# The gate products of the RG-LRU branch in the four quarters of TensorE's array

## The chip, the cores and the metric

The kernel runs on one core of a Trainium2 chip. The metric is the device time of one execution in microseconds (us). An execution is one launch of the whole network; the host only lays the data out.

## The reference

The network has two layers over 512 tokens (256 of context, 256 latent), 1024 features wide, in float32. A layer is a feed-forward half step, a mixer of three branches that run beside each other (SSD, RG-LRU and GLA), and a second feed-forward half step. The change touches the RG-LRU branch alone. Its input x, after a convolution over four tokens, is cut into 16 blocks of 64 channels. In each of two directions every block has two gates:

```
xb = x.reshape(x.shape[:-1] + (16, 64))
r = sigmoid(einsum('btnk,nkj->btnj', xb, w_a[d]).reshape(x.shape) + b_a[d])
i = sigmoid(einsum('btnk,nkj->btnj', xb, w_x[d]).reshape(x.shape) + b_x[d])
log_a = -8 * r * softplus(-lam[d])
a, b = exp(log_a), sqrt(-expm1(2 * log_a)) * (i * x)      # h[t] = a[t] * h[t-1] + b[t]
```

So there are 64x64 weight matrices, 16 of them for each gate and each direction, d = 0 forward in time and d = 1 backward. The sum of both scans times the gelu of a second input is the branch's output.

## The kernel before

Features lie on the 128 partitions and tokens along a page of 512 columns, so a tile is 128 channels, that is two blocks of the RG-LRU; there are eight tiles in a layer. The big products (`proj`, `mm3`, L360 to L365) are three matmuls each: weights and inputs are split into a rounded part and the exact rest. The weights stream in through SyncE's DMA queue; ScalarE rounds a tile of them (L333), VectorE takes the rest (L334), and TensorE reads both. A projection is 24 such matmuls into one of eight PSUM banks.

Everything smaller is background work: Python generators in a list (`start`, L755). After each projection `pump` (L774) advances them, in the list's order, until the pieces' stated costs use up a budget: 5.0 for projections of all 512 columns, 2.5 for those of the latent half alone (L799). A `yield c` ends a piece of cost c, and a `yield None` ends that generator's turn. `need` (L784) runs what is left at once. Three of the eight banks belong to background work (`B`, L208): a bank is taken from the front of the list of free ones and put back at its end. The instructions that come out so are then ordered for each engine by a planner, on its own estimates of when operands and banks are ready; so background matmuls can stand between two matmuls of a projection. On the chip each engine works through its list in order and waits where something isn't ready.

`lru_batch` (L861) is the generator changed here; one runs for two tiles. For each tile it loads the weights (L867), ends its turn, and takes four pages. Then for each direction d and each gate k it takes a bank, makes one product (L874) and one sigmoid with bias out of that bank into a page (L875), and puts the bank back; a piece ends after each direction. The 64x64 blocks of the tile's two blocks stand on the diagonal of a 128x128 matrix whose other half is zeros (`host_arrays`, L1650 to L1655). After both tiles come a tanh (L885), a product on GpSimd (L886), a square root (L890), an exponential (L894), the scans on VectorE (L909 to L914), the sum of directions (L916), the gelu's factor (L918) and the split into two parts (`hilo`, L853) that the branch's output product reads (`merge`, L1329, from the string ORDER's entry M0 on).

In layer 0 the mixer works on all columns; in layer 1 the outputs are wanted for the latent half alone, but the gates and scans of this branch still run over all 512 columns.

Of the kernel before, what the change touches and what calls it, by code (L numbers as in the profile page):

```python
# [15 lines left out]
P = 128  # L16
# [68 lines left out]
class Half:  # L85
    """Half of a page that stands for the latent columns of a whole one."""
# [10 lines left out]
class Prog:  # L97
# [9 lines left out]
    # ---------------------------------------------------------------- memory  # L107
# [42 lines left out]
    def press(self, pages, n):  # L150
        """Background work is brought forward until n pages are free."""
        while len(pages) < n and self.bg:
            t = next((t for t in self.bg if not t[2]), None)
            if t is None:
                break
            self._advance(t)
# [44 lines left out]
    def Fc(self, c0):  # L201
        """A page for the columns from c0."""
        return self.half(self.F) if c0 else self.F()
# [16 lines left out]
    def behind(self, x, first):  # L220
        """x is queued behind first, whose start flag clears all of the bank's accumulation bits."""
        if not self.dry:
            self.tc.add_manual_dep(x.ins, first.ins.name, NOSYNC, reason="same bank")
# [6 lines left out]
    # ---------------------------------------------------------------- streams  # L230
# [7 lines left out]
    def raw_issue(self, n=10 ** 6):  # L238
        """Transfers up to number n into free slots."""
        while not self.dry and self.raw_free and self.issued < min(n, len(self.plan)):  # L240
            j = self.issued
            t = self.raw_free[0]
            if j >= self.first_of.get(self.until, 10 ** 6):
                t = next((x for x in self.raw_free if all(x is not y for y in self.extra[0])), None)
                if t is None:
                    break
            self.raw_free = [x for x in self.raw_free if x is not t]
            self.raw_of[j] = t
            self.nc.sync.dma_start(self.raw_of[j], self.a["ws"][j].rearrange("p (b c) -> p b c", b=8))
            self.issued += 1  # L250

    def raw_next(self, what):
        """The next transfer's slot; raw_done follows once its reads are queued."""
        i = len(self.seq)
        self.seq.append(what)
        if self.dry:
            return Any()
        assert self.plan[i] == what, (i, self.plan[i], what)
        self.raw_issue()
        return self.raw_of[i]  # L260
# [22 lines left out]
    def more_slots(self, raw, spl):  # L283
        """Further slots, for the rest of the phase."""
# [10 lines left out]
    def retire(self):  # L295
        """The extra slots are not used again."""
# [7 lines left out]
    def pair(self, ps):  # L304
        """A weight slot from a pair of double pages."""
        return tuple(x if self.dry else x.rearrange("p a (b c) -> p (a b) c", c=P) for x in ps)

    def split_ahead(self, n):
        """Parts of the next weight tiles, tiles before number n being done: hi rounded to float32r, lo the exact rest."""
# [32 lines left out]
    def W(self, *specs, hold=0):  # L342
        """The next blocks of the weight stream, side by side: hi and lo, [128, 128 * n] each.
        hold: how many weight tiles before this one are still to be read."""
# [22 lines left out]
    # ---------------------------------------------------------------- ada  # L367
# [7 lines left out]
    def ada_first(self, q):  # L375
        """Products for shift and scale of the first layer's input, two tiles of each."""
# [12 lines left out]
    def first_u(self, q, t):  # L389
        """The modulations from those products, and the first layer's input with them, in parts."""  # L390
# [21 lines left out]
    def ffn_start(self):  # L412
        """The first six products of the first phase, contraction outermost, as the modulations come in."""
# [13 lines left out]
    def ada_begin(self, pool):  # L427
        """silu of the conditioning vectors, on every partition."""
# [8 lines left out]
    def ada_part(self, n=1):  # L437
        """n tiles of 128 modulation features each, from the rows of the transposed weights."""
# [16 lines left out]
    # ---------------------------------------------------------------- prologue  # L455
# [39 lines left out]
    # ---------------------------------------------------------------- residual and LayerNorm  # L495
    def res_begin(self, l, j, w, c0):
        """gate columns w * mods[3j + 2] for the sub-layer's output."""
# [9 lines left out]
    def res_tile(self, m, ps, halves):  # L507
        """z of tile m, from the sub-layer's output in PSUM."""
# [10 lines left out]
    def res_mean(self, halves):  # L519
        """From every z the mean over the features of its first tile is taken off; LayerNorm is blind to it."""  # L520
# [33 lines left out]
    def ln_prep(self):  # L554
        """Next modulation folded with the LayerNorm's scale and shift."""
# [16 lines left out]
    def ln_sums(self, i):  # L572
        """Sums over the tiles before the last, of half i's columns."""
# [7 lines left out]
    def ln_stats(self, i):  # L581
        """Mean and 1 / sqrt(var + eps) of half i's columns, in acc and sq[0]."""
# [22 lines left out]
    def ln_apply(self, i, q):  # L605
        """The LayerNorm over z tiles 2q and 2q + 1 of half i; then u with the next modulation, if any."""
# [34 lines left out]
    def set_cuts(self, c0):  # L641
        """The halves in use of the columns, each with its own conditioning."""
        self.halves = (1,) if c0 else (0, 1)

    def tail(self, spec, src, n):
        """The last n output tiles of a sub-layer, of the one half of the columns and then of the other."""
# [32 lines left out]
    # ---------------------------------------------------------------- first products of a phase  # L679
    def k_outer(self, spec, starts, pre):  # L680
        """Four output tiles, contraction outermost; the latent columns lag by two weight tiles."""
# [19 lines left out]
    # ---------------------------------------------------------------- feed-forward  # L701
# [4 lines left out]
    def ffn(self, l, j, c0, jm, ps=None):  # L706
        """Sub-layer jm (0 or 2) of layer l with feed-forward weights j; columns from c0 on."""
# [46 lines left out]
    # ---------------------------------------------------------------- background work  # L754
# [5 lines left out]
    def _advance(self, t):  # L760
        """One piece; its cost in microseconds of the busier vector engine, or None at a break."""
# [27 lines left out]
    # ---------------------------------------------------------------- projections  # L789
    def proj(self, specs, src, c0, ps=None, mid=None):  # L790
        """One output tile, [128 features, tokens from c0]: specs run over the contraction tiles src."""
# [17 lines left out]
    # ---------------------------------------------------------------- pieces  # L809
    def conv(self, y, ps, w, b, line, lo):  # L810
        """y = b + the four taps of ps along each line; w(k) and b are per-partition columns."""
# [13 lines left out]
    def silu2(self, out, ps, c0):  # L825
        """out = 2 silu(ps) = (tanh(ps / 2) + 1) ps"""
# [4 lines left out]
    def softplus(self, x, e, r, q, p):  # L831
        """x <- softplus(x), accurate for results near 0 too; e, r, q, p: scratch of x's shape."""
# [14 lines left out]
    def rms_scale(self, ps, n, out, c0, eps):  # L847
        """out = 1 / sqrt(ps / n + eps)"""
# [11 lines left out]
    # ---------------------------------------------------------------- RG-LRU  # L860
    def lru_batch(self, l, tiles, c0, out):  # L861
        """tiles: (number, convolved x, gelu of the gate)."""
        nc = self.nc
        st = []
        for t, xc, gl in tiles:
            w = self.F()
            nc.sync.dma_start(w, self.a["lw"][l][:, t])  # L867
            yield None
            rs = [self.F() for _ in range(4)]
            for d in range(2):  # L870
                for k, n in ((0, "lba"), (1, "lbx")):
                    ps = self.B()
                    c = (2 * d + k) * P
                    nc.tensor.matmul(ps, w[:, c:c + P], xc, start=True, stop=True)  # L874
                    nc.scalar.activation(rs[2 * d + k], ps, AF.Sigmoid,  # L875
                                         bias=self.par[l][:, PR[n] + d * 8 + t:PR[n] + d * 8 + t + 1])
                    self.fB(ps)
                yield 1.2
# [44 lines left out]
    # ---------------------------------------------------------------- SSD  # L923
    def ssd_dt(self, l, x):
        """From the biased dt rows [64 = 2 x 32, tokens]: softplus, decay sums, their columns, the sums in DRAM."""
# [189 lines left out]
    # ---------------------------------------------------------------- GLA  # L1115
    def gla_head(self, l, h, q, k, v, gs, alr, c0, out):
        """q, k: [dk, tokens]; v: per 128 tokens [tokens, 2 heads * dv]; gs: silu of the gate, 2 tiles."""
# [149 lines left out]
    # ---------------------------------------------------------------- the mixer  # L1267
# [10 lines left out]
    def mixer(self, l):  # L1278
# [18 lines left out]
        # RG-LRU  # L1297
# [28 lines left out]
        # merge  # L1326
# [60 lines left out]
        # RG-LRU and SSD, with the products of the RG-LRU branch between  # L1387
# [20 lines left out]
        # GLA, with the products of the SSD branch between  # L1408
# [92 lines left out]
    # ---------------------------------------------------------------- whole program  # L1501
    def consts2(self):
        """Per layer: 4 and -8 times softplus(-lam); the two directions' skips summed."""
# [73 lines left out]
def host_blocks(inp, specs):  # L1577
    """[128, 8, 128] of one stream tile."""
# [34 lines left out]
def feat(v):  # L1613
    """[..., n * 128] -> [128, ... * n]"""
# [4 lines left out]
def host_arrays(inp, seq):  # L1619
# [9 lines left out]
    for l in range(DEPTH):  # L1629
# [14 lines left out]
        put("lba", feat(inp["lru_b_a"][l]))  # L1644
        put("lbx", feat(inp["lru_b_x"][l]))
# [4 lines left out]
    lw = np.zeros((DEPTH, 2, 64, 8, 2, 2, 2, 64), np.float32)  # L1650
    for k, n in enumerate(("lru_w_a", "lru_w_x")):
        w = inp[n].reshape(DEPTH, 2, 8, 2, 64, 64)
        for b in range(2):
            lw[:, b, :, :, :, k, b] = w[:, :, :, b].transpose(0, 3, 2, 1, 4)
    lw = lw.reshape(DEPTH, P, 8, 4 * P)  # L1655
# [36 lines left out]
```

## Time and profile before

| | |
|---|---|
| median of 3 runs | 2749.73 us |
| lowest and highest | 2748.28 and 2752.57 us |
| profiled execution, first to last instruction (span) | 2746.5 us |
| TensorE matmuls busy | 2679.0 us, 98% |
| VectorE busy | 1935.4 us, 70% |
| ScalarE busy | 1221.4 us, 44% |
| GpSimd busy | 343.7 us, 13% |

The page gives the profiled execution's own time as its span only; the median of the runs, which were timed without a profile, is 3.2 us above that. In the rows below PE is TensorE, PEld its weight loads, DVE VectorE, ACT ScalarE, POOL GpSimd and SP SyncE; L874 is line 874 of the kernel. A float32 matmul shows as two records, a matmul on rounded parts as one. Matmuls are pipelined: the next one starts before the one before it ends, so the distance between starts tells more than a duration.

### The profile page before, as it was taken

What the parts mean: (1) busy time and instruction counts of PE and PEld (TensorE: products, weight loads), DVE (VectorE), ACT (ScalarE), POOL (GpSimd) and SP (SyncE); (2) the same over time, 40 slices, a digit from 0 to 9 for tenths busy, and PEclk for the clock granted to TensorE, in tenths of its full rate; (3) what the DMA queues carried; (4) which work ended last, traced back from release to release, by engine and by line L of the source; (5) the groups of instructions that cost most, each with busy time, mean ns of one, the idle gap of its engine ahead of it and who ended that gap; (6) DMA issues with size and microseconds to landing.
All of it is one profiled execution on the core that took longest, in us unless ns stands there. A gap on an engine that the chain in (4) does not pass through costs nothing.

```text
span 2746.5 us, 38825 instructions
## 1 busy us (share of the span) xinstructions
PE 2679.0 (98%) x14981; PEld 2280.9 (83%) x14981; DVE 1935.4 (70%) x3465; ACT 1221.4 (44%) x1745; POOL 343.7 (13%) x295
## 2 busy tenths in 40 slices
PE   7999999999999999999999999999999999999997
PEld 5888897677887888888888898888977798899997
DVE  4788769599985545458888587733598998676654
ACT  2332326863435434333323242232388655574553
POOL 0000132212210000022000230001311112002002
PEclk9999999999999999999999999999999999999999
DMA  6566534234342222234566436533333454344563
GB/s 258 184 191 195 182 122 128 71 104 138 123 135 85 74 85 77 85 103 150 185 198 199 154 108 196 180 108 107 97 117 113 135 171 132 107 139 130 169 192 116
DMA packets 117832, 380.49 MB, mean 139 GB/s; under 512 B 13888, under 2 KB 22352, under 8 KB 117648
## 3 DMA queue, kind: packets, MB, share of 16 engines
q1 hardware_dynamic: 115744, 373.00, 42.4%
q0 software_dynamic: 1472, 4.33, 0.5%
q8 instruction: 117, 1.92, 0.3%
q10 hardware_dynamic: 432, 0.69, 0.1%
q14 instruction: 67, 0.55, 0.1%
HBM read 373.63 MB, written 4.33 MB: 138 GB/s over the span
## 4 chain that ended last, share of the span: by engine, by line
PE 82%; DVE 8%; ACT 5%; issue 3%; DMA 1%; POOL 1%; SPq 0%; DVEq 0%; POOLq 0%; ACTq 0%
PE bank L362 25%; PE bank L363 25%; PE bank L364 25%; DVE wl L334 1%; DVE x L822 1%; PE bank L1233 1%; PE bank L1213 1%; PE bank L1052 1%; PE bank L874 1%; PE bank L1018 1%; PE bank L1170 1%; ACT wh L333 1%; ACT x L875 1%; PE bank L1073 0%; DVE x L908 0%
## 5 line engine op out<-in xcount | busy, mean ns | idle before, releaser
L333 ACT ACTIVATE wh<-wr 128x1024 fp32r<-128x1024 f32 x391 | 413.3, 1058 | 762.1 <-PE bank L363 519.5
L334 DVE TENSOR_TENSOR wl<-wr,wh 128x1024 fp32r<-128x1024 f32 x391 | 487.8, 1248 | 264.8 <-ACT wh L333 263.0
L444 DVE SCALAR_TENSOR_TENSOR ada_scr<-wr,sb 128x1024 f32<-128x1024 f32 x256 | 315.6, 1233 | 138.5 <-DMA wr<-in_ws_dram 135.2
L362 PE MATMUL bank<-u0h,wh 128*128 128x512 f32 (+1 forms) x660 | 246.7, 376 | 7.2 <-ACT u0h L628 3.8
L362 PE MATMUL bank<-r,wh 128*128 128x512 f32 (+1 forms) x736 | 251.6, 342 | 0.0
L364 PE MATMUL bank<-r,wl 128*128 128x512 f32 (+1 forms) x736 | 249.7, 340 | 0.0
L363 PE MATMUL bank<-r,wh 128*128 128x512 f32 (+1 forms) x736 | 249.6, 339 | 0.0
L363 PE MATMUL bank<-u0l,wh 128*128 128x512 f32 (+1 forms) x660 | 236.8, 359 | 2.1 <-DVE u0l L630 2.0
L364 PE MATMUL bank<-u0h,wl 128*128 128x512 f32 (+1 forms) x660 | 237.9, 361 | 1.0 <-DVE wl L334 0.9
L362 PE MATMUL bank<-u1h,wh 128*128 128x512 f32 (+1 forms) x660 | 234.7, 358 | 3.2 <-ACT u1h L408 2.7
L363 PE MATMUL bank<-u1l,wh 128*128 128x512 f32 (+1 forms) x660 | 233.9, 355 | 0.8 <-DVE u1l L630 0.8
L364 PE MATMUL bank<-u1h,wl 128*128 128x512 f32 (+1 forms) x660 | 234.2, 355 | 0.0
L362 PE MATMUL bank<-u2h,wh 128*128 128x512 f32 (+1 forms) x660 | 233.1, 354 | 0.0
L363 PE MATMUL bank<-u2l,wh 128*128 128x512 f32 (+1 forms) x660 | 233.0, 353 | 0.1
L364 PE MATMUL bank<-u2h,wl 128*128 128x512 f32 (+1 forms) x660 | 232.9, 353 | 0.0
L363 PE MATMUL bank<-u3l,wh 128*128 128x512 f32 (+1 forms) x644 | 228.6, 355 | 1.3 <-DVE u3l L630 1.3
L362 PE MATMUL bank<-u3h,wh 128*128 128x512 f32 (+1 forms) x644 | 228.3, 356 | 0.0
L364 PE MATMUL bank<-u3h,wl 128*128 128x512 f32 (+1 forms) x644 | 228.1, 355 | 0.0
L362 PEld LDWEIGHTS bank<-r,wh 128*128 128x128 f32 x736 | 139.4, 190 | 16.1 <-issue 1.0
L362 PEld LDWEIGHTS bank<-u0h,wh 128*128 128x128 f32 x660 | 125.8, 192 | 32.1 <-issue 6.5
L364 PEld LDWEIGHTS bank<-r,wl 128*128 128x128 f32 x736 | 139.5, 190 | 15.4 <-issue 0.3
L363 PEld LDWEIGHTS bank<-r,wh 128*128 128x128 f32 x736 | 139.5, 190 | 14.8
(502 smaller groups left out, 5911.2 us busy)
## 6 DMA issues: line engine op xcount, KB each, us to landing
wr<-in_ws_dram SPq DMA_DIRECT2D x605, 512.0 KB, 3.7
m1r<-in_ws_dram SPq DMA_DIRECT2D x29, 512.0 KB, 4.0
ada<-in_ws_dram SPq DMA_DIRECT2D x16, 512.0 KB, 9.0
x<-acs_d SPq DMA_DIRECT2D x26, 256.0 KB, 3.6
x<-acs_d SPq DMA_DIRECT2D x45, 128.0 KB, 3.5
x<-in_lw_dram SPq DMA_DIRECT2D x16, 256.0 KB, 3.6
sb<-s_d SPq DMA_DIRECT2D x6, 512.0 KB, 5.8
f<-acs_d SPq DMA_DIRECT2D x19, 128.0 KB, 3.2
```

Source lines behind the costliest of these rows:

```text
L333: nc.scalar.activation(hi, raw, AF.Copy)
L334: nc.vector.tensor_tensor(lo, raw, hi, op=ALU.subtract)
L362: x = nc.tensor.matmul(out, st[0], mv[0], start=start, stop=False, skip_group_check=True)
L363: nc.tensor.matmul(out, st[0], mv[1], start=False, stop=False, skip_group_check=True)
L364: self.last_mm = nc.tensor.matmul(out, st[1], mv[0], start=False, stop=stop, skip_group_check=True)
L444: nc.vector.scalar_tensor_tensor(self.ada_scr, raw.rearrange("p a b -> p (a b)"), 1.0, self.sb[b], op0=ALU.mult, op1=ALU.mult, accum_out=o ...
L822: nc.vector.scalar_tensor_tensor(ys[:, :, a:z], xs[:, :, a + o:z + o], w(k), ys[:, :, a:z], op0=ALU.mult, op1=ALU.add)
L874: nc.tensor.matmul(ps, w[:, c:c + P], xc, start=True, stop=True)
L875: nc.scalar.activation(rs[2 * d + k], ps, AF.Sigmoid, bias=self.par[l][:, PR[n] + d * 8 + t:PR[n] + d * 8 + t + 1])
L1018: nc.tensor.matmul(cc(ps, c), cc(Bt, c), cc(xw[d], c), start=True, stop=True, skip_group_check=True)
L1052: nc.tensor.matmul(cc(ps, c)[s], cc(Sd[d], c)[:, s], cc(Cp, c), start=True, stop=True, skip_group_check=True)
L1170: nc.tensor.matmul(cc(ps, c), cc(ki[d], c), cc(qi[d], c), start=True, stop=True, skip_group_check=True)
```

## The change

A gate k of a tile now makes four products of 64 rows by 64 columns: the forward blocks of the two 64-channel halves lie in the quarters on the array's diagonal (rows 0 to 63 to columns 0 to 63, and 64 to 127 to 64 to 127) and write bank pf; the backward blocks lie in the other two quarters and write bank pb, each half to the partitions of the other. The forward gate is one sigmoid over all partitions. The backward gate is two sigmoids of 64 partitions, which write each half to its own partitions again. The weights hold no zeros any more, a transfer is 128 KB instead of 256 KB, and the backward biases are rolled by 64 partitions on the host. Pieces end after each gate instead of each direction, at a stated cost of 1.8 instead of 1.2. The comments and docstrings of the file are blank lines now, so that the line numbers shift by at most three.

```
     def lru_batch(self, l, tiles, c0, out):
...
-            nc.sync.dma_start(w, self.a["lw"][l][:, t])
+            nc.sync.dma_start(w[:, 0:256], self.a["lw"][l][:, t])
             yield None
             rs = [self.F() for _ in range(4)]
-            for d in range(2):
-                for k, n in ((0, "lba"), (1, "lbx")):
-                    ps = self.B()
-                    c = (2 * d + k) * P
-                    nc.tensor.matmul(ps, w[:, c:c + P], xc, start=True, stop=True)
-                    nc.scalar.activation(rs[2 * d + k], ps, AF.Sigmoid,
-                                         bias=self.par[l][:, PR[n] + d * 8 + t:PR[n] + d * 8 + t + 1])
-                    self.fB(ps)
-                yield 1.2
+            lo, up = slice(0, 64), slice(64, P)
+            for k, n in ((0, "lba"), (1, "lbx")):
+                pf, pb = self.B(), self.B()
+                for ps, d, ii, oo in ((pf, 0, lo, lo), (pf, 0, up, up), (pb, 1, lo, up), (pb, 1, up, lo)):
+                    c = (2 * d + k) * 64
+                    nc.tensor.matmul(ps[oo], w[ii, c:c + 64], xc[ii], start=True, stop=True, skip_group_check=True)
+                bias = lambda d, s: self.par[l][s, PR[n] + d * 8 + t:PR[n] + d * 8 + t + 1]
+                nc.scalar.activation(rs[k], pf, AF.Sigmoid, bias=bias(0, slice(0, P)))
+                for ii, oo in ((up, lo), (lo, up)):
+                    nc.scalar.activation(rs[2 + k][oo], pb[ii], AF.Sigmoid, bias=bias(1, ii))
+                self.fB(pf, pb)
+                yield 1.8
             self.fF(w)
...
-        put("lba", feat(inp["lru_b_a"][l]))
-        put("lbx", feat(inp["lru_b_x"][l]))
+        for n, k in (("lba", "lru_b_a"), ("lbx", "lru_b_x")):
+            b = feat(inp[k][l]).copy()
+            b[:, 8:] = np.roll(b[:, 8:], 64, axis=0)
+            put(n, b)
...
-    lw = np.zeros((DEPTH, 2, 64, 8, 2, 2, 2, 64), np.float32)
-    for k, n in enumerate(("lru_w_a", "lru_w_x")):
-        w = inp[n].reshape(DEPTH, 2, 8, 2, 64, 64)
-        for b in range(2):
-            lw[:, b, :, :, :, k, b] = w[:, :, :, b].transpose(0, 3, 2, 1, 4)
-    lw = lw.reshape(DEPTH, P, 8, 4 * P)
+    lw = np.stack([inp[n].reshape(DEPTH, 2, 8, 2, 64, 64) for n in ("lru_w_a", "lru_w_x")], axis=3)
+    lw = lw.transpose(0, 4, 5, 2, 1, 3, 6).reshape(DEPTH, P, 8, 4 * 64)
```

## Rows read from the trace of the kernel before

**Rows 1.** The page: busy time by engine, and the chain that ended last, by engine.

```profile
PE 2679.0 (98%) x14981; PEld 2280.9 (83%) x14981; DVE 1935.4 (70%) x3465; ACT 1221.4 (44%) x1745; POOL 343.7 (13%) x295
...
PE 82%; DVE 8%; ACT 5%; issue 3%; DMA 1%; POOL 1%; SPq 0%; DVEq 0%; POOLq 0%; ACTq 0%
```

**Rows 2.** The chain of waits by line: 430 to 630 us, then 2005 to 2240 us.

```profile
by line: issue 12.3%; PE bank L362 7.6%; PE bank L364 7.4%; PE bank L363 7.4%; DVE x L822 5.7%; DVE wl L334 5.6%; ACT x L875 4.3%; PE bank L874 4.1%; DVE x L908 3.6%; ACT x L890 3.3%; DVE x L918 3.1%; DVE x L909 2.8%; DMA f<-acs_d 2.4%; ACT
...
by line: PE bank L362 11.2%; PE bank L363 10.7%; PE bank L364 10.6%; issue 7.1%; DVE x L822 6.4%; PE bank L874 4.7%; DVE wl L334 3.1%; DVE x L908 2.6%; DVE m1l L334 2.5%; DVE x L909 2.5%; ACT x L875 2.4%; PE bank L1018 2.4%; POOL x L916 2.2
```

**Rows 3.** Busy time of each engine in two slices of 30 us.

```profile
490.00:520.00 30.00, 28.80 (x113) 20.94 (x112) 12.20 (x18) 28.43 (x38) 5.16 (x5) 1.00 0.19 60
...
2050.00:2080.00 30.00, 28.65 (x149) 22.66 (x148) 21.87 (x41) 25.08 (x38) 6.97 (x5) 1.00 0.35 112
```

**Rows 4.** Groups by line: busy us, mean ns, idle us before and releasers.

```profile
L874 PE MATMUL bank<-x,x 128*128 128x512 f32 x128 | 64.0, 622 | 12.9 <-ACT x L953 4.9 <-ACT x L875 3.5 <-DVE x L990 3.2
...
L875 ACT ACTIVATE x<-bank,par 128x512 f32<-128x512 f32 x57 | 36.8, 686 | 6.2 <-PE bank L874 3.0 <-PE bank L364 2.2 <-POOL x L916 0.7
```

**Rows 5.** Timeline of TensorE: start us, us, line, shapes, count; gate products and projections.

```profile
436.84 2.73 PE L874 MATMUL bank<-x,x 128*128 128x512 f32 x6
...
440.73 1.12 PE L874 MATMUL bank<-x,x 128*128 128x512 f32 x2
...
446.04 3.59 PE L874 MATMUL bank<-x,x 128*128 128x512 f32 x8
...
449.70 0.40 PE L363 MATMUL bank<-u0l,wh 128*128 128x512 f32 x1
449.93 0.39 PE L364 MATMUL bank<-u0h,wl 128*128 128x512 f32 x1
...
2153.82 3.59 PE L874 MATMUL bank<-x,x 128*128 128x512 f32 x8
```

**Rows 6.** Timeline of TensorE around two groups of half-array products.

```profile
631.48 0.39 PE L364 MATMUL bank<-r,wl 128*128 128x512 f32 x1
631.80 1.09 PE L1073 MATMUL bank<-x,x 128*64 128x128 f32 x16
...
633.16 0.40 PE L362 MATMUL bank<-u0h,wh 128*128 128x512 f32 x1
...
639.07 0.39 PE L364 MATMUL bank<-u3h,wl 128*128 128x512 f32 x1
639.39 1.53 PE L1052 MATMUL bank<-x,x 128*64 128x128 f32 x24
...
641.19 0.40 PE L363 MATMUL bank<-r,wh 128*128 128x512 f32 x1
```

**Rows 7.** Single lines: count, duration ns min/median/max, first and last start.

```profile
L875 ACT ACTIVATE x<-bank,par x57: 671/687/699, 440.0 to 2149.4; 128x512 f32<-128x512 f32 x57
...
L1352 ACT ACTIVATE r<-bank x2: 590/590/591, 433.6 to 2009.2; 32x512 fp32r<-32x512 f32 x2
```

**Rows 8.** Waits of TensorE, 395 to 640 us: total us, times, longest.

```profile
PE bank L874 <- ACT x L875: 3.1, 2, 2.8
...
PE bank L362 <- ACT wh L333: 0.8, 1, 0.8
```

**Rows 9.** DMA issues: count, KB each, us to landing.

```profile
x<-in_lw_dram SPq DMA_DIRECT2D x16, 256.0 KB, 3.6
```

**Rows 10.** Timeline: last work of the branch, first product that reads it, per layer.

```profile
605.44 0.68 DVE L857 TENSOR_TENSOR r<-x,r 128x512 fp32r<-128x512 f32 x1
...
623.84 0.48 PE L362 MATMUL bank<-r,wh 128*128 128x512 f32 x1
...
2196.73 0.42 DVE L918 TENSOR_TENSOR f<-f,x 128x256 f32<-128x256 f32 x1
...
2221.05 0.28 PE L362 MATMUL bank<-r,wh 128*128 128x256 f32 x1
```

**Rows 11.** Timeline of TensorE: a gate product that waits for a bank.

```profile
479.95 2.07 PE L874 MATMUL bank<-x,x 128*128 128x512 f32 x2 [4.92 <-ACT x L953]
```

## The prediction

> **What bounds the kernel now.** I read the whole span first, then the stretches around the changed lines, then single instructions. TensorE is busy for 98% of the span, and 82% of the chain of waits is its own [rows 1], so time on TensorE is time of the kernel unless something else ends a stage. The changed code runs in two stretches, one per layer; its products (L874) start at 436.84 and end with a group at 2153.82 [rows 5]. There the picture differs. Of the chain from 430 to 630 us TensorE's projections (L362 to L364) hold only 22%, from 2005 to 2240 us 33%; the rest is split over VectorE, ScalarE and the gate products, with 4.3% (8.6 us) for the sigmoids' line L875 and 4.1% (8.2 us) for L874 [rows 2]. In the second stretch of 235 us it is 2.4% (5.6 us) and 4.7% (11.0 us) [rows 2]. TensorE is nearly full (28.80 and 28.65 us of 30 in the slices shown), and ScalarE not far from it (28.43 and 25.08) [rows 3]. So what the change takes from TensorE and what it gives to ScalarE weigh against each other in the same place.
>
> **TensorE, per product.** A product on L874 shows as two records (128 records, 64 products, four per tile of 128 channels, 16 tiles in both layers) [rows 4]. Eight records start at 446.04, and the second projection matmul behind them at 449.70; a projection matmul takes 0.23 us of the queue (449.70 to 449.93), so four products take 3.66 - 0.23 = 3.43 us, 0.86 us each [rows 5]. All 64 take 54.9 us; nothing is lost where they go in or out.
>
> A quarter product (64 rows, 64 columns) does not exist in this trace. The nearest rows are the half-array products of L1052 and L1073, 128 rows by 64 columns in alternate column halves. From the projection matmul before a group to the second one after it, less two times 0.23 us, the group of 16 records costs 633.16 - 631.48 - 0.45 = 1.23 us and the one of 24 records 641.19 - 639.07 - 0.45 = 1.67 us [rows 6]. Eight more records, which are two pairs of products, cost 0.44 us: 0.22 us a pair. A full-width product of these 128 columns would cost 0.86 / 4 = 0.21 us. So two column halves run at once, for the price of one. What is left, 1.23 - 4 x 0.22 = 0.35 us, is paid once per group for changing the shape of the array and back.
>
> Now the after side. A gate (forward and backward) becomes four quarter products of 512 columns. All at once they cost one step, 0.86 us, against 1.72 us now; as two pairs 1.72 us; one after the other 3.44 us. To this comes 0.35 us per group. I take all four at once: the quarters differ in rows or columns, the column half of this is shown above, and nothing in the trace shows the row half either way.
>
> **How the groups fall.** Background work has three PSUM banks. A product now fills one bank and the sigmoid frees it; a gate will fill two (pf, pb). A tile fills four banks before and after, and the fourth fill must wait for the first sigmoid. That is why many tiles show as six records, other work, then two (436.84 and 440.73, with ScalarE's L875 between) [rows 5]. In the timeline L874 comes in 30 groups: 5 of eight records, 7 of six, 5 of four, 13 of two. (The first and the last stand in [rows 5].) After the change such a split tile costs 0.86 + 0.86 + 0.35, later 0.86 + 0.35, together 3.28 us against 3.43 now: only 0.15 us less, because the last two quarters run without the other two. An unsplit tile costs 1.72 + 0.35 = 2.07 us: 1.36 less. A tile cut by gates costs 2.42: 1.01 less. One cut into four pairs costs 4.84: 1.41 more. Five unsplit tiles give -6.8, seven split -1.1; the other four (the groups of four and the loose twos) lie between -4.0 and +5.6, I take -1. Sum: **-9 us**, with bounds of -22 (all unsplit) and +23 (all in pairs).
>
> **ScalarE.** Per tile six sigmoids instead of four, since the backward halves go back across partitions in two instructions: 32 more. A sigmoid of 128 x 512 takes 0.687 us; a copy of 32 rows out of a bank to other partitions takes 0.590 [rows 7]. Fewer rows save little, so I take 0.64, the middle: 32 x 0.64 = +20.5 us of ScalarE. Below, it could cost nothing where ScalarE idles; above, all 20.5. Line L875 is busy for 36.8 us in its larger group, 57 of its 64 sigmoids [rows 4], so some 41 in all; 14.2 us of that stand on the chain [rows 2], a third. A third of 20.5 is **+7 us**. Queued behind the added sigmoids on ScalarE are the weight splits (L333) and behind these the projections; between 395 and 640 us TensorE already waits 0.8 us for L333 and 3.1 us for L875's release of a bank [rows 8].
>
> **The rest.** The weights' transfers shrink from 256 to 128 KB; they land in 3.6 us now [rows 9], and each is issued a pump ahead of its use: nothing. Each piece now counts 1.8 instead of 1.2 of the pump's budget, 9.6 more per layer: two pumps of 5.0 in layer 0, two to four in layer 1, where a pump has 2.5 or 5.0. A pump in layer 0 comes every 24 x 0.23 = 5.5 us, so the branch ends about 11 us later. What hides this is the gap between the last work of the branch and the first product that reads it: 606.1 to 623.8 us in layer 0, 2197.2 to 2221.1 us in layer 1 [rows 10]. Cover of 17 and 24 us; if it were gone, each microsecond over it would stand on the path. I cost it at nothing. Pages, banks and VectorE's work stay as they are. One accident near the change may go or come again: before 479.95 TensorE waits 4.92 us for a bank that L953 releases [rows 11]. In all TensorE idled 12.9 us before L874 [rows 4]; I expect as much again, give or take 8.
>
> **Sum.** -9 + 7 = -2 us. The profiled execution spans 2746.5 us, the median of the runs is 2749.73, 3.2 us above it; the sum is a difference and is laid on the median: **2748 us**. Its own range is 2735 to 2762.
>
> **Rivals.**
> *Unsplit tiles.* If the faster products let the first sigmoid come early enough, most tiles run in one group: -22 on TensorE, some +4 for ScalarE, so 2732. For it: five groups of eight now. Against it: ScalarE has a queue of 3.9 us between the first product (436.84) and the freed bank (440.73).
> *ScalarE becomes the bound (slower).* A tile comes about every 17 us (eight between 436.84 and some 574 us) and adds 1.28 us, so 2.3 us in 30, and in the slice from 490 us only 1.6 us are free [rows 3]. If all 20.5 us show, less the 9: 2761. It decides once ScalarE has under 2.3 us free in 30 us through the whole stage; the slice from 2050 us has 4.9 free [rows 3].
> By the Trainium skill ("TensorEngine Tiling (Array Packing)", section Performance Considerations, PSUM Bottleneck) emptying PSUM may become the bound once tiling makes TensorE faster; the 28.43 us of 30 agree in one slice, the 25.08 not yet in the other [rows 3].
> *Pairs only.* The row halves don't overlap: a split tile costs 1.72 + 0.86 + 0.35 and 0.86 + 0.35 = 4.14 (+0.71), an unsplit one 3.79 (+0.36): 16 x 0.4 to 0.7 = +6 to +11, with ScalarE +13 to +18: 2765.
> *The two row halves exclude each other in a bank.* Forward blocks of both row halves write one bank, though on different partitions, so I give this case little. If each had to wait for the other, a gate would be three steps (first block; second beside the third; fourth), 2.58 us against 1.72: 32 x 0.86 = 27.5, some 25 groups x 0.35 = 9, ScalarE 4: +40, 2790. With no overlap at all, 55 + 9 + 4: 2818.
> The page named above has such a rule (section Restrictions and Gotchas, PSUM Pressure): row tiles cannot use the same PSUM bank at once, and software has to see to it. No run so far shows two row halves at work.
>
> **How the numbers follow.** Forecast 0.60, unsplit 0.13, ScalarE 0.11, pairs 0.10, exclusion or no overlap 0.06. About 0.2% (5.5 us) is what a measurement can tell from none. Within the forecast's 27 us range I give 0.30 to faster, 0.50 to same, 0.20 to slower: 0.18, 0.30, 0.12. Unsplit adds 0.13 to faster; ScalarE 0.01 to same and 0.10 to slower; pairs 0.01 and 0.09; the last 0.06 to slower. Sum: faster 0.31, same 0.32, slower 0.37. Range 2731 to 2765: it leaves out the last case (0.06), the upper halves of ScalarE and pairs (0.07) and the outer edge of unsplit (0.05).
>
> **What would show it.** Right: quarter products of one gate start within a few hundredths of a microsecond and the next gate 0.43 x 2 us later; groups cost 0.86 us per gate and 0.35; six sigmoids a tile near 0.6 us; L874's successor busy for well under 64 us. Wrong: starts 0.43 us apart in twos or ones (pairs, or no overlap); ScalarE near 30 of 30 us through 440 to 570 us and projections waiting for L333; a wait before the first product that reads the branch.

## The result, and the profile after

The kernel after takes 2772.07 us (2769.69 to 2774.80, 4 runs) against 2749.78: a ratio of 1.0086, 95% interval 1.0073 to 1.0100. That is 24 us slower by the ratio, 22 by the medians. The forecast of 2748 and its range to 2765 both missed it. In this part the two profiled executions stand beside each other; they span 2746.5 and 2769.7 us.

The page of the kernel after, busy time by engine:

```profile
PE 2688.5 (97%) x15109; PEld 2270.9 (82%) x15109; DVE 1938.5 (70%) x3465; ACT 1259.6 (45%) x1786; POOL 339.5 (12%) x295
```

Against [rows 1] ScalarE is busy for 38.2 us more, nearly twice the 20.5 forecast; TensorE for 9.5 more, part of it at a lower clock (see below). Yet ScalarE is not full where the branch runs. The slice of the kernel after from 430 to 580 us, with TensorE, its weight loads, VectorE, ScalarE and GpSimd in this order (busy us and instructions):

```profile
430.00:580.00 150.00, 137.13 (x593) 90.47 (x591) 114.72 (x175) 129.23 (x170) 29.61 (x22) 0.94 0.25 83
```

The prices of the products are what the forecast said. The timeline of TensorE around the first tile, kernel after (start us, us, line, shapes, count; in brackets idle us before and who ended it), then the same view cut to 0.07 us:

```profile
436.51 0.39 PE L364 MATMUL bank<-u3h,wl 128*128 128x512 f32 x1
436.83 1.94 PE L875 MATMUL bank<-x,x 64*64 64x512 f32 x12
438.69 0.50 PE L362 MATMUL bank<-u0h,wh 128*128 128x512 f32 x1
439.03 0.40 PE L363 MATMUL bank<-u0l,wh 128*128 128x512 f32 x1
...
440.62 0.65 PE L875 MATMUL bank<-x,x 64*64 64x512 f32 x2 [0.73 <-ACT x L877]
```

```profile
436.83 0.66 PE L875 MATMUL bank<-x,x 64*64 64x512 f32 x4
```

Four records of four quarters start within 0.07 us, and twelve records (one gate whole, the forward half of the other) cost 439.03 - 436.51 - 0.45 = 2.07 us, the 0.86 + 0.86 + 0.35 of the sum to the hundredth. So all four quarters run at once, both row halves in one bank. But the last two quarters come 3.8 us later and wait for the first sigmoid. The groups of both kernels by line (busy us, mean ns, then idle us before them):

```profile
L875 PE MATMUL bank<-x,x 64*64 64x512 f32 x256 | 53.8, 643 | 14.8 <-ACT x L877 10.2 <-ACT x L956 4.4 <-ACT x L879 0.2
...
L879 ACT ACTIVATE x<-bank,par 64x512 f32<-64x512 f32 x60 | 41.0, 683 | 3.4 <-PE bank L875 2.2
L877 ACT ACTIVATE x<-bank,par 128x512 f32<-128x512 f32 x30 | 20.6, 686 | 0.6
```

The 64.0 us of [rows 4] became 53.8, but the pipelined busy time flatters. Measured as the forecast priced a group, from the projection matmul before it to the second one after it, less what those two take by themselves, and with waits and the lower clock taken off, the gate products cost TensorE 57.4 us before and 54.9 after (my sum over all records of both stretches): 2.5 us less. Sigmoids went from 36.8 us in the larger group, 57 of 64, to 41.0 + 20.6, 60 of 64 halves and 30 of 32 whole ones.

Next the waits of TensorE (total us, times, longest). Kernel after, 395 to 640 us, to be read with [rows 8]:

```profile
PE bank L364 <- DVE wl L334: 6.6, 4, 2.3
PE bank L875 <- ACT x L956: 4.4, 1, 4.4
PE bank L875 <- ACT x L877: 4.2, 3, 3.1
```

The same view from 1980 to 2380 us, first the kernel after, then the one before:

```profile
PE bank L875 <- ACT x L877: 6.0, 5, 2.1
PE bank L1055 <- DVE x L1028: 3.9, 2, 2.5
PE bank L362 <- DVE x L822: 3.0, 2, 2.4
PE bank L1076 <- POOL x L1069: 2.1, 2, 1.8
```

```profile
PE bank L874 <- DVE x L990: 3.2, 1, 3.2
PE bank L987 <- ACT x L981: 2.1, 2, 1.6
PE bank L1052 <- DVE x L1025: 1.6, 2, 1.2
```

Three kinds of wait have grown. Those for the sigmoids' banks are 4.2 and 6.0 us, against 3.1 and 0.3 before. Those for the weights' second part (L334) are 6.6 us in layer 0, against 0.9 from 430 to 640 us before. In layer 1 the SSD groups' wait for VectorE is 3.9 us, against 1.6 (L1055 is L1052 of the kernel before).

L334 reads what ScalarE's L333 has rounded, but in these four cases it was not L333 that held it up: L334 starts on VectorE without idle time, right behind other work of VectorE. (Before 507.9 us VectorE had idled 14.6 us for one rounding, so ScalarE may stand further back in the chain; how far back is open.) The timeline of VectorE before the wait of 2.24 us that ends at 571.12:

```profile
569.48 0.45 DVE L822 SCALAR_TENSOR_TENSOR x<-bank,par,x 128x255 f32<-128x255 f32 x1
569.86 1.21 DVE L334 TENSOR_TENSOR wl<-wr,wh 128x1024 fp32r<-128x1024 f32 x1
```

The longest wait for a sigmoid's bank, 3.15 us until 540.46, also leads to VectorE. The sigmoid stood behind a load of ScalarE's function table (1.28 us) and a rounding (1.04 us), and these behind an instruction of ScalarE's that had waited for VectorE's product with the gelu's factor (L921):

```profile
536.83 0.63 ACT L856 ACTIVATE r<-x 128x512 fp32r<-128x512 f32 x1 [3.79 <-DVE x L921]
```

A wait can cost twice. The timeline of TensorE after 536 us and the slices around it, kernel after (the slices' last columns: granted clock, DMA share, GB/s):

```profile
536.91 0.40 PE L362 MATMUL bank<-u1h,wh 128*128 128x512 f32 x1
540.46 1.97 PE L875 MATMUL bank<-x,x 64*64 64x512 f32 x4 [3.15 <-ACT x L877]
542.36 0.79 PE L363 MATMUL bank<-u1l,wh 128*128 128x512 f32 x1
542.95 0.63 PE L364 MATMUL bank<-u1h,wl 128*128 128x512 f32 x1
543.37 0.57 PE L362 MATMUL bank<-u1h,wh 128*128 128x512 f32 x1
```

```profile
540.40:543.70 3.30, 3.24 (x7) 1.44 (x8) 0.00 (x0) 3.20 (x6) 1.11 (x1) 0.50 0.48 159
544.00:554.00 10.00, 10.00 (x46) 8.26 (x45) 4.27 (x8) 9.94 (x14) 1.30 (x1) 1.00 0.15 52
```

After 3.15 us idle the granted clock is 0.50, that is 1.2 GHz, and matmuls start 0.42 us apart instead of 0.23.

I cut the span at the same projection matmuls in both traces, from the one at 430 us before to the one at 640, and from 2005 to 2350. Outside these stretches the two kernels gain and lose nothing over 1 us.

| us | layer 0: before, after | layer 1: before, after |
|---|---|---|
| length | 210.8, 217.2 | 344.9, 361.8 |
| TensorE waits | 12.9, 16.5 | 9.5, 19.6 |
| lost at the lower clock | 2.9, 8.0 | 1.4, 4.8 |
| gate products | 28.7, 28.0 | 28.7, 26.9 |
| projections and other products | 166.3, 164.7 | 305.2, 310.5 |

Waits and the lower clock behind them make 22 of the 23.3 us. The gate products give back 2.5 us, and the other products of layer 1 take 5.3 more; where these come from stands with full4_18_l1.

### The profile page after: what moved, and what is told of

It reads as the page before. It is cut to its first block, busy times and chain, and to the rows that moved or that the text cites. A ratio compares the mean times of both kernels' runs of the same rounds, so it can differ in the third digit from the quotient of the medians.

```text
span 2769.7 us, 39119 instructions
## 1 busy us (share of the span) xinstructions
PE 2688.5 (97%) x15109; PEld 2270.9 (82%) x15109; DVE 1938.5 (70%) x3465; ACT 1259.6 (45%) x1786; POOL 339.5 (12%) x295
## 5 line engine op out<-in xcount | busy, mean ns | idle before, releaser
L333 ACT ACTIVATE wh<-wr 128x1024 fp32r<-128x1024 f32 x391 | 413.0, 1058 | 748.0 <-PE bank L363 565.9
L334 DVE TENSOR_TENSOR wl<-wr,wh 128x1024 fp32r<-128x1024 f32 x391 | 489.4, 1252 | 281.0 <-ACT wh L333 279.5
L362 PE MATMUL bank<-u0h,wh 128*128 128x512 f32 (+1 forms) x660 | 243.3, 371 | 10.1 <-ACT u0h L628 3.8
L362 PEld LDWEIGHTS bank<-r,wh 128*128 128x128 f32 x736 | 139.5, 190 | 16.2 <-issue 0.7
L364 PEld LDWEIGHTS bank<-u0h,wl 128*128 128x128 f32 x660 | 126.5, 192 | 31.0 <-DVE wl L334 11.4
```

Source lines behind the costliest of these rows:

```text
L333: nc.scalar.activation(hi, raw, AF.Copy)
L334: nc.vector.tensor_tensor(lo, raw, hi, op=ALU.subtract)
L362: x = nc.tensor.matmul(out, st[0], mv[0], start=start, stop=False, skip_group_check=True)
L364: self.last_mm = nc.tensor.matmul(out, st[1], mv[0], start=False, stop=stop, skip_group_check=True)
```

## The experiments

Three things changed at once: the products (whole or quarter), the sigmoids (four or six a tile) and what a piece counts (1.2 or 1.8). All eight combinations were run, each beside the kernel before on the same chip. In the tables F is whole, Q is quarter products; a ratio of 1.0010 is 2.7 us.

**full4_18**

```
-                yield 1.2
+                yield 1.8
```

> The kernel before with one number changed: a piece of the gate products counts 1.8 instead of 1.2 of the pump's budget. Products and sigmoids as before. Theory pace (background work is emitted later, and the branch and the SSD groups behind it come late): at least half of the change's 22 us, 2760 to 2772 us. Theories ScalarE (32 added sigmoids) and array (quarter products cost more than they save): nothing of it, 2745 to 2755 us.

**full6_12** (kernel before)

```
-                    nc.scalar.activation(rs[2 * d + k], ps, AF.Sigmoid, bias=...)
+                    for s in ((slice(0, P),), (slice(64, P), slice(0, 64)))[d]:
+                        nc.scalar.activation(rs[2 * d + k][s], ps[s], AF.Sigmoid, bias=...)
```

> The kernel before with the backward sigmoid in two halves of 64 partitions, in place; products as before, pieces count 1.2. That is 32 more sigmoids of some 0.68 us, 21.9 us of ScalarE, and nothing else. Theory ScalarE: 2760 to 2772 us. Theories pace and array: 2747 to 2755 us.

**quart4_18** (kernel after)

```
-                for ii, oo in ((up, lo), (lo, up)):
-                    nc.scalar.activation(rs[2 + k][oo], pb[ii], AF.Sigmoid, bias=bias(1, ii))
+                nc.scalar.activation(rs[2 + k], pb, AF.Sigmoid, bias=bias(1, slice(0, P)))
```

> The kernel after with one backward sigmoid over all 128 partitions, so four sigmoids a tile; it leaves out putting the backward halves back, so the backward gates stand on the wrong channels. Theory ScalarE: the gain of the array shows alone, 2740 to 2748 us. Theory pace: 2760 to 2772 us as for the kernel after. Theory array: 2760 us or more, as it keeps the quarter products.

**quart6_12** (kernel after)

```
-                yield 1.8
+                yield 1.2
```

> The kernel after with pieces that count 1.2 instead of 1.8. Theory pace: most of the loss goes, 2750 to 2758 us. Theories ScalarE and array: it stays, 2765 to 2775 us.

**quart4_12**: the edits of quart4_18 and quart6_12 together.

> The kernel after with one backward sigmoid over all partitions (it leaves out putting the backward halves back) and with pieces that count 1.2: of the change, the quarter products alone. So far the pace alone gave +13, the added sigmoids alone +9, and taking the sigmoids off the kernel after gave -13. If the three add up, the quarter products alone give 22 less 13 less 9, that is 2745 to 2752 us. Theory ScalarE with the array's gain showing: 2740 to 2747. Theory array (they cost by themselves): 2755 or more.

**full6_18**: the edits of full6_12 and full4_18 together.

> The kernel before with both: the backward sigmoid in two halves, in place, and pieces that count 1.8; whole products. If sigmoids and pace add up: 2768 to 2775 us, as much as the kernel after, and the quarter products give nothing. If the two are one loss (work that comes late either way): 2760 to 2766, and the quarter products cost the rest.

| ratio to before (interval) | 4 sigmoids | 6 sigmoids |
|---|---|---|
| F, 1.2 | 1 | 1.0034 (1.0021 to 1.0046) |
| F, 1.8 | 1.0049 (1.0034 to 1.0064) | 1.0090 (1.0070 to 1.0111) |
| Q, 1.2 | 1.0016 (1.0006 to 1.0027) | 1.0068 (1.0053 to 1.0083) |
| Q, 1.8 | 1.0036 (1.0026 to 1.0047) | 1.0086 (1.0073 to 1.0100), the kernel after |

Going from four to six sigmoids costs 0.34, 0.41, 0.52 and 0.50%: 12 us in the mean, in every pair. The pace costs 0.49 and 0.56% with whole products, 0.20 and 0.18% with quarters: 10 us in the mean. Quarter products in place of whole ones change the time by +0.16, -0.13, +0.34 and -0.04%: a loss of 2 us in the mean, nothing like the 9 us gained in the sum. The sign seems to depend on the pace: at 1.2 they cost 4 and 9 us, clear of the intervals, at 1.8 they save 4 and 1, within them. full6_18, without one quarter product, is as slow as the kernel after.

**full4_09, full4_15**: is it lateness, or does any other interleaving cost?

```
-                yield 1.2
+                yield 0.9        # full4_09; 1.5 in full4_15
```

> The kernel before with pieces that count 0.9 instead of 1.2. Theory pace (what counts more comes later, and late is what costs): 2742 to 2751 us, no loss. Rival, chance (any other interleaving of background work loses some waits that this one happens to avoid): 2754 to 2765 us.

> The kernel before with pieces that count 1.5, half way to 1.8. Theory pace: half of the 13 us, 2754 to 2759 us. Rival, chance: anything between 2748 and 2770 us, not in order with 1.2 and 1.8.

1.0018 (1.0009 to 1.0028) and 1.0054 (1.0039 to 1.0069). Neither theory holds whole: from 1.5 on the loss is complete, so it is no slope, and 0.9 loses 5 us too. So the kernel before stands at a good interleaving. How much of the loss at 1.8 is only that, these two runs don't show.

**full4_18_l1, full4_18_l0**: the 1.8 in one layer alone (`yield 1.8 if l else 1.2`, and the reverse).

> The kernel before with pieces that count 1.8 in layer 1 alone. If the loss arises in layer 1, as the places where full4_18 falls behind say: 2760 to 2765 us. If the two layers share it: 2753 to 2758.

> The same in layer 0 alone. If the loss arises in layer 1: 2747 to 2752 us. If the layers share it: 2753 to 2758.

1.0055 (1.0038 to 1.0071) in layer 1, 1.0005 (0.9996 to 1.0015) in layer 0. With whole products and four sigmoids the pace's loss is all in layer 1. There a pump has 2.5 for most projections. The last sigmoids, in full4_18_l1 and then in the kernel before (count: ns min/median/max, first and last start us):

```profile
L875 ACT ACTIVATE f<-bank,par x4: 677/684/690, 2159.6 to 2179.8; 128x512 f32<-128x512 f32 x4
```

```profile
L875 ACT ACTIVATE f<-bank,par x7: 668/689/702, 2103.2 to 2158.0; 128x512 f32<-128x512 f32 x7
```

They come 22 us later, and what stands behind them in the list moves with them: counted in projection matmuls, half of the SSD scores (L1063) are done some 70 matmuls later than before (9803 against 9733), the last of them at the same place (10,070 against 10,068). The same SSD work is pressed into fewer projections, and TensorE waits for it: in the kernel after L1055 for VectorE and L1076 for GpSimd, shown above. That the pressing causes these waits is argued from the order, not tried by itself.

A second part can be counted. Nearly all of layer 1's products on half the array (128 rows by 64 columns) belong to the SSD, and each group of them changes the shape of the array, the 0.35 us that the forecast had found. In the stretch of layer 1 the same 200 records come in 28 groups in the kernel before, in 42 in full4_18 and full4_18_l1, in 37 in full6_12 and in 41 in the kernel after. With the groups grows what TensorE spends outside gate products, waits and the lower clock: 305.2 us with 28, 307.7 with 37, 310.3 with 42 (full4_18) and 310.5 with 41 (the kernel after). So some 5 us of full4_18's 14 in this stretch are changes of shape; 5 more are waits, and 4 the lower clock.

**full4_b4, quart4_b4, quart6_b4**: does the array's gain show once banks suffice?

```
-NBG = 3
+NBG = 4        # kernel before; quart4_12; quart6_12
```

> The kernel before with four PSUM banks instead of three for background work (NBG = 4), so that a tile's four products need not wait for the tile's own first sigmoid. It is the base for the next two. Whole products cost 3.43 us a tile however they are grouped, so what changes is the interleaving and the waits for banks: 2740 to 2765 us, no theory says more.

> The quarter products alone (four sigmoids, the backward halves are not put back; pieces count 1.2) with four background banks. Theory banks (the last two quarters of a tile run alone because three banks are too few): a tile now costs 2.07 us in one group instead of 3.43, so up to 16 x 1.36 = 22 us less than the same kernel with whole products and four banks, at least 8. Rival, nothing to win (TensorE in this stage waits for ScalarE and VectorE anyway, and what the array saves turns into waits): within 4 us of it.

> The same with the backward sigmoid in two halves, which put the halves back: the whole change, but for the pace, with four background banks. Theory ScalarE: the added 21.9 us of sigmoids cost 9 to 14 us over the run with four sigmoids, as with three banks. Rival (what they cost was the fourth bank's wait for the first sigmoid): under 4 us over it.

1.0047 (1.0032 to 1.0062), 1.0040 (1.0025 to 1.0055) and 1.0090 (1.0074 to 1.0107). The timeline of TensorE around one tile of quart4_b4:

```profile
446.19 0.39 PE L364 MATMUL bank<-u3h,wl 128*128 128x512 f32 x1
446.51 1.95 PE L875 MATMUL bank<-x,x 64*64 64x512 f32 x16
448.39 0.50 PE L362 MATMUL bank<-u0h,wh 128*128 128x512 f32 x1
448.72 0.40 PE L363 MATMUL bank<-u0l,wh 128*128 128x512 f32 x1
```

A whole tile in 448.72 - 446.19 - 0.45 = 2.08 us, against 3.43 for whole products [rows 5]; most tiles run so. The products' groups by line, in full4_b4, quart4_b4 and, with three banks, quart4_12:

```profile
L874 PE MATMUL bank<-x,x 128*128 128x512 f32 x128 | 61.6, 615 | 5.7 <-ACT x L953 4.1 <-ACT x L981 1.1 <-DVE x L990 0.5
```

```profile
L875 PE MATMUL bank<-x,x 64*64 64x512 f32 x256 | 39.6, 624 | 3.4 <-ACT x L955 2.1 <-DVE x L992 0.9 <-ACT x L877 0.4
```

```profile
L875 PE MATMUL bank<-x,x 64*64 64x512 f32 x256 | 53.1, 637 | 16.6 <-ACT x L877 7.8 <-ACT x L955 4.9 <-DVE x L992 3.6
```

Measured as above the products fall from 56.8 us in full4_b4 to 40.3 in quart4_b4, 16 us; the time falls by 2 (2760.52 to 2758.40), and the two intervals overlap. In the two stretches waits and clock took all of it: waits 10.1 + 11.9 against 14.4 + 18.2 us, clock 1.6 + 5.1 against 9.4 + 3.4. What TensorE waits for from 430 to 640 us, in full4_b4 and in quart4_b4:

```profile
PE bank L364 <- DVE wl L334: 4.1, 5, 2.4
```

```profile
PE bank L364 <- DVE wl L334: 8.8, 5, 3.1
```

And from 2005 to 2365 us, in the same order:

```profile
PE bank L362 <- DVE x L822: 1.8, 3, 1.2
```

```profile
PE bank L362 <- DVE x L822: 8.1, 5, 4.2
```

So the rival of that experiment stands. In layer 0 TensorE waits longer for the second part of the weights, in layer 1 for the convolution (L822), which reads a projection's bank. Both are VectorE's work, and what the array saves becomes waiting. The six sigmoids cost 14 us here too (1.0040 to 1.0090), with the fourth bank's wait gone.

**after_round_pool**: a direct attempt to take work off ScalarE.

```
-POOL_HI = (0, 0)
+POOL_HI = (1, 1)        # kernel after
```

> The kernel after with every fourth weight tile of the two stages rounded on GpSimd instead of ScalarE (POOL_HI = 1): takes some 13 of 52 roundings of 1.06 us a stage off ScalarE, about what the sigmoids add. Theory ScalarE (its queue is what costs): 4 to 12 us less than the kernel after, 2760 to 2768 us. Rivals pace and array: no gain, 2768 to 2780 us, the more so as GpSimd takes some 4 us for what ScalarE does in one.

1.0128 (1.0113 to 1.0143), 10 us over the kernel after: the theory's forecast of a gain missed. ScalarE's busy time did fall, from 1259.6 to 1226.1 us, but a rounding takes GpSimd 2.94 us, and VectorE's L334 sat idle for 30.2 us until such roundings were done. The waits for the sigmoids' banks grew too, from 430 to 640 us to 6.1 us against 4.2. So the run swaps one delay for another; which of them costs the 10 us is open, and it can't decide on ScalarE's time. The rounding's line in after_round_pool:

```profile
L331 POOL TENSOR_SCALAR wh<-wr 128x1024 fp32r<-128x1024 f32 x21 | 61.7, 2940 | 103.1 <-PE bank L363 53.7 <-DVE x L1086 26.2 <-DVE x L902 11.6
```

**full_cols, full_less**: ScalarE's time, or one more instruction?

```
-                    nc.scalar.activation(rs[2 * d + k], ps, AF.Sigmoid, bias=...)
+                    for s in ((slice(0, T),), (slice(0, TL), slice(TL, T)))[d]:     # full_less: the first half alone
+                        nc.scalar.activation(rs[2 * d + k][:, s], ps[:, s], AF.Sigmoid, bias=...)
```

> The kernel before with the backward sigmoid in two halves of 256 columns and all partitions, instead of two halves of 64 partitions: as many instructions as in full6_12, but a 256-column activation out of a bank takes 0.38 us against 0.69 for 512, so some 2 to 4 us of ScalarE are added instead of 21.9. Theory ScalarE's time: 2747 to 2752 us. Rival, another order (any added instruction shifts the interleaving): 2756 to 2763 us, as full6_12.

> The kernel before with the backward sigmoids over 256 of the 512 columns; the other columns are left out (GpSimd writes a constant there). As many sigmoids as before, some 10 us less of ScalarE. Theory ScalarE's time (it binds the stage): 2742 to 2747 us, 2 to 6 less than before. Rival, another order: 2751 to 2760 us.

0.9996 (0.9987 to 1.0006) and 0.9983 (0.9973 to 0.9992). Thirty-two more sigmoids cost nothing when they are cut by columns, and 9 us when they are cut by partitions (full6_12). With less of ScalarE's work than before (and a constant written by GpSimd), the kernel is 4 us faster. The pages of full6_12, full_cols and full_less:

```profile
PE 2690.1 (98%) x14981; PEld 2285.6 (83%) x14981; DVE 1940.8 (70%) x3465; ACT 1243.0 (45%) x1776; POOL 347.0 (13%) x295
```

```profile
PE 2681.2 (98%) x14981; PEld 2282.0 (83%) x14981; DVE 1935.7 (70%) x3465; ACT 1223.0 (44%) x1775; POOL 341.4 (12%) x295
```

```profile
PE 2679.3 (98%) x14981; PEld 2282.5 (83%) x14981; DVE 1937.2 (71%) x3465; ACT 1214.6 (44%) x1745; POOL 353.3 (13%) x327
```

ScalarE's busy time against the 1221.4 us of [rows 1]: +21.6, +1.6 and -6.8 us; the time of the kernel: +9, 0 and -4 us. The theory of ScalarE's time stands, the rival (another order) falls for these kernels. By which waits ScalarE's time becomes the kernel's is not shown one by one; those followed above run through VectorE too.

**full4_b4_first, full4_b4_first5**: the one place where four banks were faster.

```
+        self.bank_list = list(self.banks)
...
+        if l == 0:
+            self.bgbanks = {id(x) for x in self.bank_list[:4]}
         for x in ORDER[l].split():
+            if x == "S0":
+                self.bgbanks = {id(x) for x in self.bank_list[:NBG]}
```

> The kernel before with a fourth background bank only while the gate products of layer 0 are made (until ORDER's first S0), where full4_b4 was 5 us shorter between 430 and 580 us. If that gain stands alone: 2742 to 2746 us. If what follows gives it back, as in full4_b4: 2748 to 2756 us.

> The same kernel as full4_b4_first, in five rounds. If its 2.5 us are real: a ratio of 0.998 to 0.9995 with an interval below 1. If not: an interval that holds 1.

0.9991 (0.9982 to 1.0001) and, in five rounds, 0.9992 (0.9983 to 1.0001). Both times some 2 us, both times the interval holds 1: not settled. No version here is shown to beat the kernel before, except full_less, which leaves part of the gates out.

## Why the prediction was wrong

- **The array.** Right in its prices: four quarters at once (0.86 us a gate), 0.35 us a group, 2.07 us for twelve records. Wrong in "Sum: **-9 us**": TensorE's cost fell by 2.5 us, and the time rose by 2 in the mean of the four pairs. The count of groups was taken from the kernel before, and a tile that ran in one group was priced as if all four quarters of its second gate met. With three banks the fourth fill waits for the first sigmoid in nearly every tile, and TensorE, being faster, comes to that wait sooner (10.2 us of waits for L877 against 3.5 for L875 in [rows 4]). So 30 groups became 34. And where banks do suffice the 16 us saved become waits and lower clock. [Rows 2] had said so: the projections held 22 and 33% of the chain there, so a term of TensorE's could not count in full.
- **ScalarE.** Mis-sized: "32 x 0.64 = +20.5 us of ScalarE" is 38.2 us by the pages, and "+7 us" is 12. Of the 38.2 some 27 are the sigmoids: the duration of one (0.68 us, near the 0.64 foreseen) hid that sigmoids overlap, see the last section. The other 11.5 are nine more loads of ScalarE's function tables (109 against 100, 1.28 us each). They come with the two edits together: full6_18 has seven more, full4_18 none and full6_12 one less. The share of ScalarE's time that shows, a third in the forecast, was about right: 9 of 21.6 us in full6_12.
- **The pace.** "I cost it at nothing" failed, 13 us alone and 10 us in the mean. I asked whether the branch itself would be late. It was not: in the kernel after its last work ends at 2223.1 and the first product that reads it starts at 2235.0, a cover of 12 us where there had been 24 [rows 10]. What became late was the work behind it in the list, and it was cut into more groups: 14 more changes of the array's shape, some 5 us. That change was priced at 0.35 us for the gate products and forgotten for the SSD's.
- **The rivals.** "ScalarE becomes the bound" named the side, at 2761 us and 0.11, but its condition was not met: ScalarE had 20.8 us free of the 150 shown above, 4.2 in 30, and not under 2.3. The added sigmoids cost time although ScalarE was not full. The page of the Trainium skill behind that rival ("TensorEngine Tiling (Array Packing)", section Performance Considerations, PSUM Bottleneck) says that emptying PSUM may become the bottleneck once TensorE is faster. This case agrees in part: with four banks 16 us of the array's moved the time by 2, and the waits that grew were in layer 1 for VectorE's reading of a projection's bank, but in layer 0 for the weights. "Pairs only" and the exclusion of row halves in one bank are refuted by the four records that start within 0.07 us and the 0.86 us that four quarters cost. The same page of the Trainium skill (section Restrictions and Gotchas, PSUM Pressure) rules out two row tiles in one bank at once; here, where the two halves write different partitions of the bank, no such wait showed.
- **Range and chances.** The failed terms all lean one way (+11, +5, +10 us), and I had treated them as if they could offset each other.

## What to carry to other kernels

A faster product is worth what the stage lets through: look first at which engine ends the waits there, and price a saving on another engine at nothing. Count a change of the array's shape for every group of products that the new order cuts apart, not only for those that were edited. When a change cuts an instruction in two, price the cut by the distance between starts, not by a duration, and prefer a cut along columns to one along partitions if both serve. A cost that only paces a list of background work is an edit to the schedule of everything behind it; test it alone.

## What the runs showed that I had not expected

Two sigmoids over 64 partitions each cost ScalarE more than twice one over all 128. The timeline of ScalarE in the kernel before, then in the kernel after:

```profile
439.98 1.84 ACT L875 ACTIVATE x<-bank,par 128x512 f32<-128x512 f32 x3
```

```profile
439.88 0.69 ACT L877 ACTIVATE x<-bank,par 128x512 f32<-128x512 f32 x1
440.59 1.38 ACT L879 ACTIVATE x<-bank,par 64x512 f32<-64x512 f32 x2
441.99 0.69 ACT L877 ACTIVATE x<-bank,par 128x512 f32<-128x512 f32 x1
```

Three whole ones take 1.84 us, so they start (1.84 - 0.69) / 2 = 0.57 us apart, each while the one before still runs. Around the halves the starts are 0.70 us apart, with no overlap. Per tile that is 6 x 0.70 = 4.2 us against 4 x 0.57 = 2.3, 30 us over 16 tiles where every sigmoid stands next to another. Halves by columns keep the overlap: in full_cols two whole ones and four halves take 2.74 us together, the halves some 0.37 us from start to start. The row of full_cols, then two of full6_12:

```profile
440.20 2.74 ACT L876 ACTIVATE x<-bank,par 128x512 f32<-128x512 f32 x6
```

```profile
439.23 4.08 ACT L876 ACTIVATE x<-bank,par 128x512 f32<-128x512 f32 x6
443.20 0.71 ACT L886 ACTIVATE x<-x,spl 128x512 f32<-128x512 f32 x1
```

full6_12 writes its halves in place and loses the overlap between them too, so the crossing of partitions isn't the cause. Nor is the small number of partitions: the last half of full6_12's six, partitions 0 to 63, ends at 443.31, 0.11 us after the whole instruction behind it has started. What the pairs without overlap have in common is that the second instruction begins at another partition than the first. The kernel before had shown it. L1349 is on partitions 0 to 63, L1351 on 64 to 127, and L1352 reads from 64 and writes from 0:

```profile
431.37 1.06 ACT L333 ACTIVATE wh<-wr 128x1024 fp32r<-128x1024 f32 x1 [1.47 <-PE bank L363]
432.34 0.67 ACT L1349 ACTIVATE x<-bank,par 64x512 f32<-64x512 f32 x1
433.03 0.59 ACT L1351 ACTIVATE r<-bank 64x512 fp32r<-64x512 f32 x1
433.64 0.59 ACT L1352 ACTIVATE r<-bank 32x512 fp32r<-32x512 f32 x1
```

L1349 starts 0.09 us before L333 ends, though it has half the partitions; L1351 and L1352 start after the end of the one before. The rule isn't settled: the instruction behind L1352 reads from partition 0 again and does overlap, and no run changed the first partition alone.
